# A second buffer for the second pair of weight sums (R) of gate and up

## The chip, the cores and the metric

The kernel runs on one core of one Trainium2 chip. The metric is the device time of one execution in microseconds. A core has engines that work side by side, each through its own instructions in order: TensorE (PE, with its weight loads PEld), VectorE (DVE), ScalarE (ACT), GpSimd (POOL), and SyncE (SP), which here only issues DMAs. They wait for each other through semaphores.

## The reference

One layer of a decoder: a mixer (a state space branch beside a gated delta rule branch), and then a dense SwiGLU block. The change touches only the two first products of that block, gate and up:

```
x = x + rms_norm(mix, norm_mix_post)
f = rms_norm(x, norm_ffn_pre)
f = (silu(f @ w_ffn_gate) * (f @ w_ffn_up)) @ w_ffn_down
x = x + rms_norm(f, norm_ffn_post)
```

There are 2048 prompt tokens and 32 sample tokens, 1024 features, and 2816 hidden columns. The 16 meta tokens run through the mixer only.

## The kernel before

The program is written with tiles and pools. A pool gives each tag a number of buffers; a tile that finds no free buffer waits until the last reader of the oldest one is done. A scheduler then sets the order of the instructions on each engine from the order of the program, the readiness that it computes, and the buffers that are free. So the number of buffers changes not only waits but also the order in which an engine does its work; engines never leave that order on the chip.

**Stages.** Phase one (projections, state space, delta rule) takes the first half of the span. `merge` and `way_out` follow, where the last token tiles are normed, turned to features and written to `f_d`. Then `gate_up` reads `f_d` and writes the hidden rows to `h_d`, and `down` multiplies these by `w_ffn_down`.

**Numbers in two parts.** Each factor of a product is held as a rounded part (`hi`, made by ACT in `fp32r`) and a remainder (`lo`, made by DVE or POOL as the difference). `mm3` (L155) therefore issues three matmuls for one: L158, L159, L160.

**gate_up.** Gate and up are computed by Strassen's scheme in Winograd's form: seven products of half blocks in place of eight. The activations come in three pairs of column blocks of width 348, 348 and 344 (`PAIRS`), the weights in 11 blocks of 256 hidden columns; 33 steps in all. A step of `gate_up_step` does 14 products, seven for gate (i = 0) and seven for up (i = 1), each of 4 x 3 matmuls: 168 matmuls. In the order of the program, with PSUM sums Y, X and Z for each i:

1. Y0 with a11, X0 with a12, Y1 with a11, X1 with a12 (products 1 to 4)
2. Y0 and Y1 with s2 added (5, 6), Z0 with s1 (7), Y0 with s3 added (8), Z1 with s1 (9), Y1 with s3 added (10)
3. Y0 with a22 added (11), Z0 with s4 added (12), Y1 with a22 added (13), Z1 with s4 added (14)

Between the products `snap` (L1537, tile `sn`, ACT) copies a sum out of PSUM before more is added to it; `plus` (L1541, tile `su`, DVE) adds such a copy to another sum; `gated` makes silu with a tanh on ACT (L1546, tile `th`) and a product on DVE (L1547); and `hm` is the hidden row, finished by POOL (L1565, L1579, L1592) or DVE (L1585) and stored by SP (L1550).

**a_parts** prepares the weights of the next step, spread through the present one by `fac()`. For gate and for up it loads the raw block `araw` (1 MB, L1483, two buffers, one each), and makes from it

- a11 and a12: rounded by ACT (L1476, tile `ah`), remainder by DVE (L1477, tile `al`)
- `early(i)`: four sums of 128 x 512 on DVE, S in two halves (L1489, L1490) and R in two halves (L1491, L1492), then s2 and s1 from S (rounded by ACT, remainder by DVE)
- `late(i)`: s3 and s4 from R, and a22 from the raw block (rounded by ACT, remainder by POOL)

The program calls early(0), early(1), late(0), late(1). S and R are tiles of the pool `gs` (L1733), which has one buffer for each tag. R of up can then be written only when `late(0)` has read R of gate, and R of gate for the next step only when `late(1)` has read R of up. The parts s3, s4 and a22 of one i have one buffer as well, so `late(i)` of the next step begins when PE has used the parts of the present one.

Of the kernel before, what the change touches and what calls it, by code (L numbers as in the profile page):

```python
# [7 lines left out]
F32 = mybir.dt.float32  # L8
# [7 lines left out]
P = 128  # L16
# [34 lines left out]
def ap_of(t, off, dims):  # L51
    return bass.AP(tensor=t.tensor, offset=t.offset + off, ap=[list(d) for d in dims])
# [19 lines left out]
class Trunk:  # L72
# [730 lines left out]
    def gdn_special(self):  # L803
# [10 lines left out]
        qn = self.q_norm(sq, SPC)  # L814
        R = slice(32, SPC)

# [19 lines left out]
        for h in range(H):  # L836
            nc.tensor.matmul(pt[R, h], ks[:, h, 1], self.ident, start=True, stop=True)
            nc.tensor.matmul(po[R, h], ks[:, h, 0], self.ident, start=True, stop=True)
        r = self.g2("r")[:SPC]
        v.tensor_copy(r, vc)  # L840
        o = self.g2("o")
        for h in range(H):
            v.scalar_tensor_tensor(r[R, h], pt[R, h], self.c1[R, 0, h:h + 1], vc[R, h], op0=OP.mult, op1=OP.add)
        v.tensor_tensor(o[R], po[R], self.egc[R, 0, :, None].to_broadcast([32, H, P]), op=OP.mult)
        pv = self.gp.tile([P, H, P], F32, tag="gp", name="pv")[:SPC]
# [9 lines left out]
        for h in range(H):  # L855
            nc.tensor.matmul(po[:SPC, h], qk[:, h], vt[:, h], start=True, stop=True)
        v.tensor_add(o[R], o[R], po[R])

# [608 lines left out]
    def a_parts(self, s, out):  # L1467

        nc, v, gp = self.nc, self.nc.vector, self.nc.gpsimd
        flat = lambda t: t.rearrange("p a k m -> p (a k) m")  # L1470
        def parts(i, names, x, eng):
            n = len(names)
            pool = {"a11": self.ae, "s2": self.am[i]}.get(names[0], self.ar)
            hi = pool.tile([P, n, 4, P], F32R, tag=f"{names[0]}{i}h", bufs=1, name="ah")
            lo = pool.tile([P, n, 4, P], F32R, tag=f"{names[0]}{i}l", bufs=1, name="al")
            nc.scalar.activation(flat(hi), x, AF.Copy)  # L1476
            eng.tensor_sub(flat(lo), x, flat(hi).bitcast(F32))  # L1477
            for j, nm in enumerate(names):
                out[i][nm] = hi[:, j], lo[:, j]
        raws, sums = [], [None] * 2  # L1480
        for i, w in enumerate((self.w_fg, self.w_fu)):
            raw = self.gr.tile([P, 8, 256], F32, tag="raw", name="araw")
            nc.sync.dma_start(raw, ap_of(w, 256 * s, [[FF, P], [P * FF, 8], [1, 256]]))  # L1483
            raws.append(raw)
        def early(i):
            a, c = raws[i][:, :, 0:P], raws[i][:, :, P:256]
            S = self.gs.tile([P, 2, 4, P], F32, tag="S", name="S")
            R = self.gs.tile([P, 2, 4, P], F32, tag="R", name="R")
            v.tensor_add(S[:, 1], c[:, 0:4], c[:, 4:8])  # L1489
            v.tensor_sub(S[:, 0], S[:, 1], a[:, 0:4])  # L1490
            v.tensor_sub(R[:, 0], a[:, 0:4], c[:, 0:4])  # L1491
            v.tensor_sub(R[:, 1], a[:, 4:8], S[:, 0])  # L1492
            parts(i, ("s2", "s1"), flat(S), v)
            sums[i] = flat(R)
        def late(i):
            parts(i, ("s3", "s4"), sums[i], gp)
            parts(i, ("a22",), raws[i][:, 4:8, P:256], gp)
        for i in range(2):
            parts(i, ("a11", "a12"), raws[i][:, :, 0:P], v)
            yield  # L1500
        for f in (early, late):
            for i in range(2):
                f(i)
                yield
# [452 lines left out]
```

## Time and profile before

| what | value |
|---|---|
| time, median of 3 runs | 3268.27 us (3264.24 to 3269.39) |
| the profiled execution | 3277.85 us, its span 3275.8 us |
| mean granted TensorE clock | 0.972 |
| gate and up, first to last matmul into `psf` | 1819.8 to 2750.8 us |
| in it: matmuls L158, L159, L160 | 1848 each |
| R's sums L1491, L1492 | 62 each, 128 x 512 |

The profile has one execution. Its page lists busy times by engine, and groups of instructions by line with the idle time of the engine ahead of them and what ended that. Views of the trace give the waits (who waited for whom, total, times, longest), the timeline (start, duration, engine, line, operation, tiles, and in brackets the idle time before it and its releaser) and windows (busy time of each engine in a stretch, with the granted clock and the DMA share). In names, `psf<-xh,ah` reads output from inputs; numbers of buffers are left out, so gate's and up's tiles have one name. Matmuls overlap: one takes some 0.32 us from begin to end, and the next begins after half of that. A releaser is the event that came last by the profile.

### The profile page before, as it was taken

The page shows a single profiled execution, that of the slowest core. Times are in us where ns is not written, and L with a number is a line of the kernel's source. Part 1 is how long each engine was busy: PE and PEld are TensorE (multiplying, and loading weights), DVE is VectorE, ACT ScalarE, POOL GpSimd, SP SyncE. Part 2 cuts the span into 40 slices and gives each one's busy share as a digit, 9 for nine tenths or more (in the row PEclk, how much of TensorE's full clock was granted, in tenths as well). Part 3 has the DMA queues.
Part 4 walks back from the last instruction along what each step waited for, and adds up shares of the span by engine and source line. Part 5 has one row for each costly group of instructions (what it writes and reads, how often), then busy time and mean ns, then how long its engine had stood idle before and what let it go on. Part 6 is the DMA issues. An engine that isn't in the chain of part 4 may idle for free. (4 is left out here: it accounts for less than half of the span.)

```text
span 3275.8 us, 47596 instructions
## 1 busy us (share of the span) xinstructions
PE 3108.8 (95%) x17461; PEld 2729.7 (83%) x17461; DVE 2028.0 (62%) x4674; ACT 1116.7 (34%) x1952; POOL 908.7 (28%) x907
## 2 busy tenths in 40 slices
PE   7998999999989999999999799999999999999998
PEld 6887787877777888888777699999999998888886
DVE  6888854557788645644455766676676664236235
ACT  4643222433333224211243444344444443213211
POOL 1134431112332211201211344434434443212110
PEclk8998998999999999999999899999999999999999
DMA  4335556545556645544555433333332334326223
GB/s 119 120 105 161 145 147 169 121 104 139 158 173 182 168 114 143 165 137 127 181 180 172 149 104 104 104 118 99 100 97 89 102 103 139 125 82 162 78 64 69
DMA packets 460553, 419.30 MB, mean 128 GB/s; under 512 B 112330, under 2 KB 384906, under 8 KB 460320
## 3 DMA queue, kind: packets, MB, share of 16 engines
q1 hardware_dynamic: 450048, 382.18, 40.0%
q0 software_dynamic: 10272, 34.09, 3.8%
q8 instruction: 137, 2.24, 0.3%
q14 instruction: 96, 0.79, 0.1%
HBM read 288.27 MB, written 127.65 MB: 127 GB/s over the span
## 5 line engine op out<-in xcount | busy, mean ns | idle before, releaser
L158 PE MATMUL psf<-xh,ah 128*128 128x348 f32 (+1 forms) x1848 | 598.3, 324 | 27.0 <-ACT sn L1537 20.1
L160 PE MATMUL psf<-xh,al 128*128 128x348 f32 (+1 forms) x1848 | 594.3, 322 | 1.5 <-POOL al L1477 1.5
L159 PE MATMUL psf<-xl,ah 128*128 128x348 f32 (+1 forms) x1848 | 592.9, 321 | 0.0
L145 POOL TENSOR_TENSOR wu<-wr,wu 128x512 fp32r<-128x512 f32 x136 | 218.2, 1607 | 667.5 <-ACT wu L143 618.0
L158 PEld LDWEIGHTS psf<-xh,ah 128*128 128x128 f32 x1848 | 348.4, 189 | 36.5 <-ACT sn L1537 28.7
L160 PEld LDWEIGHTS psf<-xh,al 128*128 128x128 f32 x1848 | 347.9, 188 | 1.8 <-POOL al L1477 1.7
L159 PEld LDWEIGHTS psf<-xl,ah 128*128 128x128 f32 x1848 | 347.9, 188 | 0.0
L158 PE MATMUL psg<-pgh,wu 128*128 128x512 f32 (+2 forms) x800 | 299.6, 374 | 1.2 <-ACT gt L1218 1.2
L1642 PE MATMUL psr<-wu,hh 128*128 128x512 f32 (+2 forms) x748 | 292.4, 391 | 3.7 <-POOL wu L145 3.7
L1641 PE MATMUL psr<-wu,hh 128*128 128x512 f32 (+2 forms) x748 | 290.8, 390 | 2.3 <-ACT wu L143 2.3
L160 PE MATMUL psg<-pgh,wu 128*128 128x512 f32 (+2 forms) x800 | 288.7, 361 | 4.0 <-DVE wu L146 4.0
L159 PE MATMUL psg<-pgl,wu 128*128 128x512 f32 (+2 forms) x800 | 288.0, 360 | 0.0
L1644 PE MATMUL psr<-wu,hl 128*128 128x512 f32 x704 | 274.7, 391 | 0.0
L146 DVE TENSOR_TENSOR wu<-wr,wu 128x512 fp32r<-128x512 f32 x136 | 121.8, 897 | 137.6 <-ACT wu L143 137.2
L143 ACT ACTIVATE wu<-wr 128x1024 fp32r<-128x1024 f32 x136 | 142.6, 1054 | 140.3 <-DMA wr<-w_ffn_down 58.6
L158 PE MATMUL psq<-pgh,wu 128*128 128x512 f32 (+2 forms) x480 | 184.5, 384 | 3.7 <-ACT gt L1218 3.1
L158 PEld LDWEIGHTS psg<-pgh,wu 128*128 128x128 f32 x800 | 154.8, 194 | 29.4 <-issue 9.4
L160 PEld LDWEIGHTS psg<-pgh,wu 128*128 128x128 f32 x800 | 154.8, 194 | 27.0 <-DVE wu L146 4.2
L159 PE MATMUL psq<-pgl,wu 128*128 128x512 f32 (+2 forms) x480 | 175.3, 365 | 0.0
L160 PE MATMUL psq<-pgh,wu 128*128 128x512 f32 (+2 forms) x480 | 174.7, 364 | 0.0
L1477 POOL TENSOR_TENSOR al<-R,ah 128x1024 fp32r<-128x1024 f32 x62 | 162.0, 2613 | 38.5 <-ACT ah L1476 38.5
L159 PEld LDWEIGHTS psg<-pgl,wu 128*128 128x128 f32 x800 | 154.8, 193 | 18.8 <-issue 0.2
(495 smaller groups left out, 6721.1 us busy)
## 6 DMA issues: line engine op xcount, KB each, us to landing
wr<-w_in SPq DMA_DIRECT2D x72, 512.0 KB
araw<-w_ffn_gate SPq DMA_DIRECT2D x31, 1024.0 KB
araw<-w_ffn_up SPq DMA_DIRECT2D x31, 1024.0 KB
wr<-w_ffn_down SPq DMA_DIRECT2D x44, 512.0 KB
zg_d<-gt SPq DMA_DIRECT2D x80, 256.0 KB
h_d<-hm SPq DMA_DIRECT2D x44, 348.0 KB
qkv_d<-cy SPq DMA_DIRECT2D x48, 256.0 KB
hr<-h_d SPq DMA_DIRECT2D x16, 768.0 KB
```

Source lines behind the costliest of these rows:

```text
L143: nc.scalar.activation(hi[:, :n], raw[:, :n], AF.Copy)
L145: nc.gpsimd.tensor_sub(lo[:, :c], raw[:, :c], hi[:, :c].bitcast(F32))
L146: nc.vector.tensor_sub(lo[:, c:n], raw[:, c:n], hi[:, c:n].bitcast(F32))
L158: t.matmul(ps, wh, xh, start=first, stop=False, **kw)
L159: t.matmul(ps, wh, xl, start=False, stop=False, **kw)
L160: t.matmul(ps, wl, xh, start=False, stop=last, **kw)
L1477: eng.tensor_sub(flat(lo), x, flat(hi).bitcast(F32))
L1641: nc.tensor.matmul(ps, hi[:, k, cl], wh[:, cs], start=k == 0, stop=False)
L1642: nc.tensor.matmul(ps, hi[:, k, cl], wl[:, cs], start=False, stop=both and k == n - 1)
L1644: nc.tensor.matmul(ps, lo[:, k, c - c0:c - c0 + r], wh[:, cs], start=False, stop=k == n - 1)
```

## The change

R gets two buffers in place of one. Sums, roundings, products and transfers stay the same in kind, number and size.

```diff
         def early(i):
             a, c = raws[i][:, :, 0:P], raws[i][:, :, P:256]
             S = self.gs.tile([P, 2, 4, P], F32, tag="S", name="S")
-            R = self.gs.tile([P, 2, 4, P], F32, tag="R", name="R")
+            R = self.gs.tile([P, 2, 4, P], F32, tag="R", bufs=2, name="R")
             v.tensor_add(S[:, 1], c[:, 0:4], c[:, 4:8])
             v.tensor_sub(S[:, 0], S[:, 1], a[:, 0:4])
             v.tensor_sub(R[:, 0], a[:, 0:4], c[:, 0:4])
             v.tensor_sub(R[:, 1], a[:, 4:8], S[:, 0])
```

The pool `gs` grows by 4 KB in each partition. The scheduler's order changes at three places.

**DVE, from the end of one step into the next**, in the steady part of the stage. `th_19313` belongs to the end of the step; `araw_19128` is up's raw block and R_19267 up's R for the step that begins; `araw_19392` and `araw_19394` are gate's and up's raw blocks for the step after it, R_19496 and R_19533 their R; `su_19432` adds X0 of the step that begins. Before:

```order
L1547 SCALAR_TENSOR_TENSOR th_19313<-th_19313,su_19311 128x348
L1491 TENSOR_TENSOR R_19267<-araw_19128 128x512
L1492 TENSOR_TENSOR R_19267<-araw_19128,S_19266 128x512
L1585 TENSOR_TENSOR hm_19097<-th_19296,psf_19134 128x348
L1541 TENSOR_TENSOR su_19350<-psf_19239,sn_19200 128x348
L1489 TENSOR_TENSOR S_19495<-araw_19392 128x512
L1490 TENSOR_TENSOR S_19495<-S_19495,araw_19392 128x512
L1491 TENSOR_TENSOR R_19496<-araw_19392 128x512
L1492 TENSOR_TENSOR R_19496<-araw_19392,S_19495 128x512
L1541 TENSOR_TENSOR su_19432<-psf_19379,sn_19377 128x348
L1477 TENSOR_TENSOR al_19397<-araw_19392,ah_19396 128x1024
L1547 SCALAR_TENSOR_TENSOR th_19434<-th_19434,su_19432 128x348
```

The same place with the change:

```order
L1547 SCALAR_TENSOR_TENSOR th_19313<-th_19313,su_19311 128x348
L1585 TENSOR_TENSOR hm_19097<-th_19296,psf_19134 128x348
L1541 TENSOR_TENSOR su_19350<-psf_19239,sn_19200 128x348
L1489 TENSOR_TENSOR S_19495<-araw_19392 128x512
L1491 TENSOR_TENSOR R_19496<-araw_19392 128x512
L1490 TENSOR_TENSOR S_19495<-S_19495,araw_19392 128x512
L1492 TENSOR_TENSOR R_19496<-araw_19392,S_19495 128x512
L1541 TENSOR_TENSOR su_19432<-psf_19379,sn_19377 128x348
L1491 TENSOR_TENSOR R_19533<-araw_19394 128x512
L1477 TENSOR_TENSOR al_19397<-araw_19392,ah_19396 128x1024
L1547 SCALAR_TENSOR_TENSOR th_19434<-th_19434,su_19432 128x348
```

Up's R (R_19267) has left this place; it was done earlier in the step. Where, the next one (R_19533) shows: its first half comes right behind the `su` of X0, and its second half follows in the middle of the step, behind up's S and ahead of the remainder of up's S.

**SP, the loads and stores of one step.** `araw_19392` is gate's raw block, `araw_19394` up's; `hm_19097` is the hidden row that DVE ends (L1585), `hm_19096` the one that POOL ends (L1592). Before:

```order
L1483 DMA araw_19392<-w_ffn_gate 128x8x256
L1483 DMA araw_19394<-w_ffn_up 128x8x256
L1550 DMA h_d_70<-hm_19097 128x696
L1550 DMA h_d_70<-hm_19096 128x696
L1483 DMA araw_19658<-w_ffn_gate 128x8x256
```

With the change:

```order
L1483 DMA araw_19392<-w_ffn_gate 128x8x256
L1550 DMA h_d_70<-hm_19097 128x696
L1483 DMA araw_19394<-w_ffn_up 128x8x256
L1550 DMA h_d_70<-hm_19096 128x696
L1483 DMA araw_19658<-w_ffn_gate 128x8x256
```

Up's load stands behind the first store and ahead of the second one.

**ACT, at the start of the stage**, where the last token tiles of `way_out` (`sq`, and `fo` from the transposes `pst`) run beside the first step of `gate_up`; the first `ah<-S` here is gate's. Before:

```order
L1440 ACTIVATE xh<-t_17704 128x1392
L1476 ACTIVATE ah<-S 128x1024
L274 ACTIVATE fo<-pst,smalls 128x128 x4
L1440 ACTIVATE xh<-fr 128x1392 x3
L1537 ACTIVATE sn<-psf 128x348 x3
L1440 ACTIVATE xh<-t_17704 128x1392
L1546 ACTIVATE th<-su 128x348
L1393 ACTIVATE sq,wss<-xr 128x1024
L274 ACTIVATE fo<-pst,smalls 128x128 x8
L1476 ACTIVATE ah<-S 128x1024
L1476 ACTIVATE ah<-R 128x1024
```

With the change:

```order
L1440 ACTIVATE xh<-t_17704 128x1392
L1440 ACTIVATE xh<-fr 128x1392
L274 ACTIVATE fo<-pst,smalls 128x128 x4
L1440 ACTIVATE xh<-fr 128x1392 x2
L1537 ACTIVATE sn<-psf 128x348 x2
L1393 ACTIVATE sq,wss<-xr 128x1024
L1440 ACTIVATE xh<-t_17704 128x1392
L1546 ACTIVATE th<-su 128x348
L274 ACTIVATE fo<-pst,smalls 128x128 x8
L1476 ACTIVATE ah<-S 128x1024
L1476 ACTIVATE ah<-R 128x1024
```

Gate's first S is now rounded behind the last `fo` instead of ahead of the first ones; on DVE the first S and R of gate and up have moved behind the norm of the last token tile (L1410), and on PE the two products that use gate's S there (Y0 with s2, Z0 with s1) behind that tile's eight transposes. On the other engines and in all steps after the second the order of PE, ACT and POOL is the same in both kernels.

## The prediction

> **What bounds the kernel now.** I read the page from the top: span, busy times, then the costliest groups.
>
> ```profile
> span 3275.8 us, 47596 instructions
> PE 3108.8 (95%) x17461; PEld 2729.7 (83%) x17461; DVE 2028.0 (62%) x4674; ACT 1116.7 (34%) x1952; POOL 908.7 (28%) x907
> L158 PE MATMUL psf<-xh,ah 128*128 128x348 f32 (+1 forms) x1848 | 598.3, 324 | 27.0 <-ACT sn L1537 20.1
> ```
>
> The kernel is bound by TensorE (PE), and nothing here adds or removes a matmul. All that the change can win is time in which PE stands still in the gate and up stage; the third row says that there is some, 27.0 us ahead of the first matmul of a triple, 20.1 of it ended by the snapshot `sn`. How full is PE otherwise? The windows view of a stretch of the stage, and of one of the down stage behind it (columns: PE, PEld, DVE, ACT, POOL busy, clock, DMA):
>
> ```profile
> 2200.00:2300.00 100.00, 97.79 (x608) 96.68 (x607) 68.13 (x83) 40.96 (x64) 46.04 (x26) 1.00 0.36 113
> 2860.00:2960.00 100.00, 100.00 (x443) 82.81 (x442) 39.72 (x51) 20.96 (x21) 19.38 (x11) 1.00 0.32 99
> ```
>
> PE is idle 2.2% in gate and up, at full clock; and the down stage shows that a PE busy for all of 100 us keeps its clock at 1.00, so filling the gaps need not cost clock. Who makes the gaps? The view of waits of that stage, total, times, longest:
>
> ```profile
> PE psf L158 <- ACT sn L1537: 20.1, 31, 1.6
> ACT th L1546 <- DVE su L1541: 168.5, 68, 5.3
> DVE R L1491 <- POOL al L1477: 66.6, 29, 2.3
> ```
>
> 31 waits, about one for each of the stage's 33 steps. Read upward they look like a chain, but totals don't prove one; the timeline of one step does (start, duration, engine, line, idle before it):
>
> ```profile
> 2088.20 0.38 SPq L1483 DMA_DIRECT2D araw<-w_ffn_gate  x1
> 2089.22 2.40 POOL L1477 TENSOR_TENSOR al<-R,ah 128x1024 fp32r<-128x1024 f32 x1 [1.04 <-ACT ah L1476]
> 2089.50 2.49 DVE L1547 SCALAR_TENSOR_TENSOR th<-th,su 128x348 f32<-128x348 f32 x1 [0.85 <-ACT th L1546]
> 2091.92 1.78 DVE L1491 TENSOR_TENSOR R<-araw 128x512 f32<-128x512 f32 x1
> 2093.62 0.68 DVE L1492 TENSOR_TENSOR R<-araw,S 128x512 f32<-128x512 f32 x1
> 2094.36 0.38 SPq L1483 DMA_DIRECT2D araw<-w_ffn_up  x1
> 2094.65 0.51 DVE L1541 TENSOR_TENSOR su<-psf,sn 128x348 f32<-128x348 f32 x1
> 2095.08 0.68 DVE L1489 TENSOR_TENSOR S<-araw 128x512 f32<-128x512 f32 x1
> 2095.23 1.32 POOL L1592 TENSOR_TENSOR hm<-th,su 128x348 f32<-128x348 f32 x1 [2.10 <-DVE su L1541]
> 2096.51 2.86 POOL L1477 TENSOR_TENSOR al<-R,ah 128x1024 fp32r<-128x1024 f32 x1
> 2099.41 0.69 DVE L1491 TENSOR_TENSOR R<-araw 128x512 f32<-128x512 f32 x1 [2.30 <-POOL al L1477]
> 2100.01 0.68 DVE L1492 TENSOR_TENSOR R<-araw,S 128x512 f32<-128x512 f32 x1
> 2100.62 0.51 DVE L1541 TENSOR_TENSOR su<-psf,sn 128x348 f32<-128x348 f32 x1
> 2101.16 0.49 ACT L1546 ACTIVATE th<-su 128x348 f32<-128x348 f32 x1 [4.40 <-DVE su L1541]
> 2101.19 0.32 PE L160 MATMUL psf<-xh,al 128*128 128x348 f32 x1
> 2101.56 0.44 ACT L1537 ACTIVATE sn<-psf 128x348 f32<-128x348 f32 x1
> 2101.90 1.05 ACT L1476 ACTIVATE ah<-araw 128x1024 fp32r<-128x1024 f32 x1
> 2102.06 0.43 PE L158 MATMUL psf<-xh,ah 128*128 128x348 f32 x1 [0.56 <-ACT sn L1537]
> 2102.32 0.32 PE L159 MATMUL psf<-xl,ah 128*128 128x348 f32 x1
> 2113.80 0.32 PE L159 MATMUL psf<-xl,ah 128*128 128x348 f32 x1
> 2129.67 0.43 PE L158 MATMUL psf<-xh,ah 128*128 128x348 f32 x1 [0.54 <-ACT sn L1537]
> ```
>
> From below: PE at 2102.06 adds the sixth product into up's sum, which `sn` must first have copied. ACT could have copied it long before, but stood 4.40 us in front of `th`, whose input `su` is late; `su` is late because DVE, which works in order, waited 2.30 us in front of gate's R. That R waited for the one buffer, which up's R of the step before held until POOL had read it (2096.51 + 2.86). And that read is late because up's R was written only at 2091.92, behind POOL's reading of gate's R. So the one buffer makes gate and up take turns, and a turn is too long for the step by a little.
>
> **The price of the wait.** Between matmuls lie (2113.80 - 2102.32)/72 = 0.1594 us, so a step of 168 should take 26.79 us. It takes 2129.67 - 2102.06 = 27.61: 0.82 us lost, 0.71 as the gap itself (2101.19 to 2102.06, less one beat) and 0.1 as the slow restart (2102.06 to 2102.32). In the third pair of columns (width 344):
>
> ```profile
> 2680.07 0.42 PE L158 MATMUL psf<-xh,ah 128*128 128x344 f32 x1 [0.72 <-ACT sn L1537]
> 2680.33 0.32 PE L159 MATMUL psf<-xl,ah 128*128 128x344 f32 x1
> 2691.63 0.32 PE L159 MATMUL psf<-xl,ah 128*128 128x344 f32 x1
> 2707.46 0.42 PE L158 MATMUL psf<-xh,ah 128*128 128x344 f32 x1 [0.72 <-ACT sn L1537]
> ```
>
> a beat is 11.30/72 = 0.157, a step should be 26.37 and is 27.39: 1.02 lost. Of the 31 waits 22 lie in the first two pairs and 9 in the third: 22 x 0.82 + 9 x 1.02 = **27.2 us**, all that can be won in the steady steps. The least that the same rows allow, the bare idle time, is 20.1.
>
> **The change part by part.** No instruction is added or taken away; 31 x 4 sums, roundings and remainders are done as before. Three things move.
>
> *R no longer takes turns.* By the order, DVE now does after up's last product `hm`, `su`, then S, R, S, R of gate (four sums), then `su` of gate, then the first sum of up's R. When does `su` begin, and when must it? Its followers take 0.54 (to `th`), 0.40 (to `sn`) and 0.50 (to PE) by the rows above, 1.44 in all. PE would be ready at 2101.19 + 0.16 = 2101.35, so `su` must begin by 2099.91; now it is 2100.62, 0.71 too late, which is the gap. Up's R (1.70 + 0.60) has left the place ahead of `hm`, so DVE is ready for S at about 2092.8. S needs gate's load, issued at 2088.20. What a load takes is seen where one is waited for:
>
> ```profile
> 1853.34 0.37 SPq L1483 DMA_DIRECT2D araw<-w_ffn_gate  x1
> 1858.92 0.71 DVE L1489 TENSOR_TENSOR S<-araw 128x512 f32<-128x512 f32 x1 [1.03 <-DMA araw<-w_ffn_gate]
> ```
>
> 5.6 us, so S begins at 2093.8. Four sums at 0.60 each (2099.41 to 2100.01) give `su` at 2096.2. A sum beside a busy POOL takes up to 1.70 (2091.92 to 2093.62); four such give 2100.6, no better than now. I take a value between: POOL has two instructions there, the end of `hm` (0.7 at most after 2093.8) and up's remainder (2.40 at 2089.22), and each can hold up one sum, not four: 2093.8 + 2.4 + 3.1 = 2099.3 at the latest, 0.6 us before the limit, 3.7 at the earliest. So the gap closes in every such step, and what is late next has more room: ACT's `sn` is then bound by its own product.
>
> The row of 2089.50 shows this hold-up: `th` took 2.49 us and ended 0.37 after POOL's read of gate's R (2089.22 + 2.40); the sums at 2099.41 and 2100.01, with POOL idle, took 0.69 and 0.68. [...]
>
> *Up's first sum and its load.* That sum now stands ahead of gate's a11 remainder, `th` and up's `su` on DVE and waits for up's load. On SP that load is now queued behind the store of the first `hm`, not ahead of both stores:
>
> ```profile
> araw<-w_ffn_up SPq DMA_DIRECT2D x31, 1024.0 KB
> h_d<-hm SPq DMA_DIRECT2D x44, 348.0 KB
> ```
>
> The store waits for `hm`, which comes 2.3 us earlier since up's R left the place ahead of it; so I let the load go out no later than today's 2094.36, beside a store of 348 KB. At 5.6 x 1372/1024 = 7.5 us (an estimate by bytes) it lands by 2101.9. DVE may stand there up to 5 us; behind it wait only POOL's `hm` and remainders for the next step, and DVE is busy 68 of 100 us. What PE could notice is ACT's rounding of up's a11 (2101.90), since the snapshot of gate's sum stands behind it. It is due before the eighth product, at 2101.35 + 2 x 1.91 = 2105.2; less 1.05, 0.44 and 0.50 the load may land at 2103.2. Cost: nothing, with 1.3 us to spare.
>
> *The start of the stage.* The allocator's larger pool moves the first S and R behind the last token tile's norm, as the order of ACT shows, and two products with them. Here the trace has
>
> ```profile
> 1848.63 0.66 PE L158 MATMUL psf<-xh,ah 128*128 128x348 f32 x1 [6.48 <-ACT ah L1476]
> 1859.14 0.43 PE L160 MATMUL psf<-xh,al 128*128 128x348 f32 x1 [1.45 <-POOL al L1477]
> ```
>
> PE waits here until 1848.63 anyway. Doing two products (2 x 1.91 us) only after that would lose 3.8 us. Against this DVE reaches the end of that norm with some 4.8 us less work ahead of it (six sums of 0.6 and a remainder of 1.2 leave their place), and the wait of 1.45 for R's turn goes. I take 0, between a loss of 4 and a gain of 6.
>
> **Sum.** 3277.85 (the profiled execution: its span of 3275.8 and 2 us around it) - 27 = 3251. That execution lies 9.6 us above the median of the runs, so for the median 3268.27 - 27 = **3241 us**. With 20.1 to 27.2 for the steps and -4 to +6 for the start its own range is 3235 to 3252.
>
> **Rivals.** *POOL's hold-up eats it* (chance 0.12): if more than two of the four sums are held up, `su` begins between 2099.9 and 2100.6 and a part of the gap stays; half of it gives 3268 - 13.6 = 3255. For it: R took 1.78 and `th` 2.49 in the rows above. Against it: POOL has only two instructions in that stretch.
>
> *Another wait takes its place* (0.07): PE's gap is closed by another cause of the same length, or the two snapshots at the changes of pairs stay and the start loses 4 and more: 3262 to 3274, no change. Against it: the group's 27.0 us of L158 are 20.1 for `sn` and 6.48 in the start; there is 0.4 left for anything else.
>
> *Up's load comes too late* (0.05), and the kernel is slower: the load, now behind a store, lands after 2103.2; then ACT's rounding holds the snapshot and PE waits at the eighth product. At 2104.1 the loss equals the 0.82 of today; at 2105.0 it is 31 x 1.8 = 56 us, less the 27: 3268 + 29 = 3297. For it: the order on SP. Against it: the load would need 10.6 us from today's issue, and 5.6 was seen.
>
> That the change does nothing is excluded, as DVE's order is another one.
>
> **Chances and range.** Forecast 0.76, part 0.12, no change 0.07, slower 0.05. The forecast's 3235 to 3252 with the partial case to 3257 holds about 0.8. Faster by over 0.2% (6.5 us, about what a measurement of this kernel can tell from no change): 0.88; within: 0.07; slower: 0.05.
>
> **What will show it.** Right: the row "PE psf L158 <- ACT sn" falls from 31 waits to a few, "DVE R L1491 <- POOL al" from 66.6 us to near nothing, a step of the second pair takes 26.8 us, and windows of the stage show PE above 99%. R L1491 may wait for "DMA araw<-w_ffn_up" instead, at no cost. Wrong: a period that stays at 27.6; a new releaser ahead of L158, L159 or L160; a first wait in the stage that ends later than 1848.63 by more than 4 us; or a clock under 1.00 once PE has no gaps.

## The result, and the profile after

| | before | changed |
|---|---|---|
| median, us | 3266.26 (3263.95 to 3269.39, 4 runs) | 3239.36 (3235.94 to 3243.47, 4 runs) |
| profiled execution, its span | 3277.85, 3275.8 | 3235.94, 3233.8 |
| first to last matmul into `psf` | 930.98 | 904.28 |
| the same, first two steps | 78.14 | 77.84 |

The ratio is 0.9907 (95% interval 0.9891 to 0.9924): faster by 26.9 us at the medians. The two spans differ by more, 42 us, but 15 of these lie ahead of the stage: the first matmul into `psf` starts at 1804.81 in place of 1819.79, in a part of the program where the order is the same, so that is the run and not the change (in the traces of the thirteen kernels of the table below that matmul starts between 1803.99 and 1819.79 us, with one buffer or two). Therefore the stage itself, first to last matmul into `psf`, from start to start, is what I compare below; steps are read by taking every 168th matmul of it. From the page of the changed kernel, and its windows view of the stretch that the prediction quotes:

```profile
span 3233.8 us, 47558 instructions
PE 3087.9 (95%) x17461; PEld 2720.1 (84%) x17461; DVE 2049.3 (63%) x4674; ACT 1126.3 (35%) x1952; POOL 895.9 (28%) x907
L158 PE MATMUL psf<-xh,ah 128*128 128x348 f32 (+1 forms) x1848 | 595.3, 322 | 8.2 <-ACT ah L1476 5.1
2200.00:2300.00 100.00, 100.00 (x629) 100.00 (x628) 72.36 (x85) 44.13 (x66) 45.43 (x27) 1.00 0.37 114
```

PE now does 629 matmuls in 100 us in place of 608, at full clock; the 27.0 us of idle time ahead of L158 have become 8.2, all in the first step. The waits of the stage:

```profile
PE psf L158 <- ACT sn L1537: 1.1, 1, 1.1
ACT th L1546 <- DVE su L1541: 119.6, 66, 4.8
DVE S L1489 <- DMA araw<-w_ffn_gate: 25.7, 29, 2.6
DVE R L1491 <- DMA araw<-w_ffn_up: 6.6, 13, 1.4
```

PE's 31 waits for the snapshot are one, and R's wait for POOL (66.6 us) is gone from the list. `th` still waits 119.6 us for `su`, which now costs nothing. One step, from the timeline (it starts at 2231.14, the sixth product at 2240.72):

```profile
2227.59 0.37 SPq L1483 DMA_DIRECT2D araw<-w_ffn_gate  x1
2230.96 1.57 POOL L1477 TENSOR_TENSOR al<-araw,ah 128x512 fp32r<-128x512 f32 x1
2231.83 0.33 SPq L1550 DMA_DIRECT2D h_d<-hm  x1
2232.50 0.93 POOL L1592 TENSOR_TENSOR hm<-th,su 128x348 f32<-128x348 f32 x1
2232.56 0.37 SPq L1483 DMA_DIRECT2D araw<-w_ffn_up  x1
2233.06 0.91 DVE L1489 TENSOR_TENSOR S<-araw 128x512 f32<-128x512 f32 x1 [0.83 <-DMA araw<-w_ffn_gate]
2233.39 2.85 POOL L1477 TENSOR_TENSOR al<-R,ah 128x1024 fp32r<-128x1024 f32 x1
2233.89 2.89 DVE L1491 TENSOR_TENSOR R<-araw 128x512 f32<-128x512 f32 x1
2236.71 0.68 DVE L1490 TENSOR_TENSOR S<-S,araw 128x512 f32<-128x512 f32 x1
2237.43 0.69 DVE L1492 TENSOR_TENSOR R<-araw,S 128x512 f32<-128x512 f32 x1
2238.04 0.51 DVE L1541 TENSOR_TENSOR su<-psf,sn 128x348 f32<-128x348 f32 x1
2238.58 0.50 ACT L1546 ACTIVATE th<-su 128x348 f32<-128x348 f32 x1 [2.46 <-DVE su L1541]
2238.83 0.69 DVE L1491 TENSOR_TENSOR R<-araw 128x512 f32<-128x512 f32 x1 [0.28 <-DMA araw<-w_ffn_up]
2238.98 0.44 ACT L1537 ACTIVATE sn<-psf 128x348 f32<-128x348 f32 x1
2240.72 0.32 PE L158 MATMUL psf<-xh,ah 128*128 128x348 f32 x1
```

Gate's R no longer waits for POOL before it starts. It takes 2.89 us instead, and ends half a microsecond behind POOL's instruction that began before it; the other three sums take 0.68 to 0.91. Even so `su` starts 6.90 us into the step, where it started 8.85 us into it before. The snapshot ends at 2239.42; PE needs it 1.24 us later (2240.72, less the 0.06 from the end of a snapshot to the matmul).

Every step of the first two pairs from the second on now takes 26.81 us, every step of the third 26.41. Before, an ordinary step of the first two pairs took 27.6 (27.9 in a few), one of the third 27.39; the second step and the last one of a pair took longer (29.4 and 28.5), and the one behind a change of pairs already ran at 26.81 or 26.41.

### The profile page after: what moved, and what is told of

Read it like the earlier page. It is cut to its first block, busy times and chain, and to the rows that moved or that the text cites. A ratio compares the mean times of both kernels' runs of the same rounds, so it can differ in the third digit from the quotient of the medians.

```text
span 3233.8 us, 47558 instructions
## 1 busy us (share of the span) xinstructions
PE 3087.9 (95%) x17461; PEld 2720.1 (84%) x17461; DVE 2049.3 (63%) x4674; ACT 1126.3 (35%) x1952; POOL 895.9 (28%) x907
## 4 chain that ended last, share of the span: by engine, by line
PE 61%; issue 14%; DVE 14%; DMA 6%; POOL 3%; ACT 2%; SPq 1%; POOLq 0%; DVEq 0%; ACTq 0%
PE psf L160 9%; PE psf L158 9%; PE psf L159 9%; PE psg L158 2%; PE psr L1642 2%; PE psr L1644 2%; PE psg L160 2%; PE psr L1641 2%; PE psg L159 2%; DVE cy L386 2%; DMA wr<-w_ffn_down 1%; PE psq L158 1%; PE psq L160 1%; PE psq L159 1%; DVE bt L625 1%
## 5 line engine op out<-in xcount | busy, mean ns | idle before, releaser
L158 PE MATMUL psf<-xh,ah 128*128 128x348 f32 (+1 forms) x1848 | 595.3, 322 | 8.2 <-ACT ah L1476 5.1
L158 PEld LDWEIGHTS psf<-xh,ah 128*128 128x128 f32 x1848 | 348.8, 189 | 9.4 <-ACT ah L1476 5.8
L158 PE MATMUL psg<-pgh,wu 128*128 128x512 f32 (+2 forms) x800 | 301.2, 376 | 1.2 <-ACT gt L1218 1.2
L158 PE MATMUL psq<-pgh,wu 128*128 128x512 f32 (+2 forms) x480 | 183.4, 382 | 4.3 <-ACT gt L1218 3.8
L158 PEld LDWEIGHTS psg<-pgh,wu 128*128 128x128 f32 x800 | 155.8, 195 | 26.6 <-issue 6.1
```

The costliest lines, as they stand in the source:

```text
L158: t.matmul(ps, wh, xh, start=first, stop=False, **kw)
```

## The experiments

All medians and ratios are against runs of the kernel before on the same chip; the stage and the steps are from one trace of each (us). Medians of kernels whose stages agree within 1 us differ by up to 5, as the part ahead of the stage varies from run to run, so the stage is the finer measure.

| kernel | median | ratio, 95% interval | stage | first two steps | a step of pair two / three |
|---|---|---|---|---|---|
| before | 3264.43 to 3268.88 in the four groups | 1 | 930.98 | 78.14 | 27.63 / 27.39 |
| changed | 3239.36 | 0.9907, 0.9891 to 0.9924 | 904.28 | 77.84 | 26.81 / 26.41 |
| s_two | 3264.90 | 0.999, 0.998 to 1.0 | 929.82 | 77.24 | 27.63 / 27.39 |
| pad | 3266.62 | 0.9994, 0.9984 to 1.0004 | 929.44 | 77.12 | 27.63 / 27.39 |
| r_apart | 3242.05 | 0.9917, 0.9902 to 0.9932 | 903.65 | 77.21 | 26.81 / 26.41 |
| sn_first | 3244.72 | 0.9925, 0.991 to 0.9939 | 904.85 | 78.33 | 26.81 / 26.41 |
| dve | 3238.91 | 0.9912, 0.9898 to 0.9925 | 901.53 | 75.09 | 26.81 / 26.41 |
| pool2b | 3382.94 | 1.0349, 1.0321 to 1.0377 | 1046.07 | 84.75 | 30.04 to 32.63 / 31.2 to 32.6 |
| su1 | 3240.20 | 0.9914, 0.99 to 0.9927 | 903.59 | 76.57 | 26.81 / 26.41 |
| su2 | 3241.68 | 0.9915, 0.9901 to 0.9929 | 904.99 | 78.49 | 26.81 / 26.41 |
| sd2 | 3250.18 | 0.9952, 0.9932 to 0.9972 | 913.56 | 79.43 | 27.12 / 26.41 |
| pool2 | 3271.70 | 1.0015, 1.0002 to 1.0028 | 936.38 | 78.48 | 27.82 / 27.57 |
| load | 3246.83 | 0.9926, 0.9913 to 0.994 | 907.02 | 76.95 | 26.81 / 26.41 to 27.58 |

### Is it R's buffer? (s_two, pad, r_apart)

**s_two**, the second buffer for S:

```diff
-            S = self.gs.tile([P, 2, 4, P], F32, tag="S", name="S")
+            S = self.gs.tile([P, 2, 4, P], F32, tag="S", bufs=2, name="S")
             R = self.gs.tile([P, 2, 4, P], F32, tag="R", name="R")
```

> S gets the second buffer in place of R. Theory: R still takes turns, R L1491 still waits for POOL some 60 us in all and PE for the snapshot in about 31 steps of 27.6 us; with the start as in the padded kernel 3268, ratio 1.0005. Rival (any looser buffer of the sums, or the other order that it brings, closes the gap): near 3239, ratio 0.992.

Its waits:

```profile
DVE R L1491 <- POOL al L1477: 69.3, 30, 2.7
PE psf L158 <- ACT sn L1537: 20.4, 31, 2.2
```

As the theory had it: the wait for POOL and the 31 waits of PE stay. A second buffer for S is worth nothing here.

**pad**, one buffer, and an unused tile of R's size in the pool:

```diff
-            R = self.gs.tile([P, 2, 4, P], F32, tag="R", name="R")
+            R = self.gs.tile([P, 2, 4, P], F32, tag="R", name="R"); self.gs.tile([P, 2, 4, P], F32, tag="pad", name="pad")
```

> R has one buffer, and the pool gs gets an unused tile of the size of R, so the start of the stage is ordered as with the change, and the steady steps as before. Theory: the wait of R for POOL and PE's gap of 0.82 us stay in every step, the first step takes some 51 us: 2.3 us over the kernel before, near 3268.5, ratio 1.0007. Rival (the place in memory or the start makes the gain): near 3239, ratio 0.992.

The steady steps stay at 27.63 and 27.39, so a larger pool without a second R makes no gain in them. The other half of the expectation failed: the first two steps take 77.12 us, 1.0 less than before and not 2.3 more.

**r_apart**, a buffer each for gate and up, and the start ordered as before:

```diff
-            R = self.gs.tile([P, 2, 4, P], F32, tag="R", name="R")
+            R = (self.gs, self.ar)[i].tile([P, 2, 4, P], F32, tag="R", bufs=1, name="R")
```

> Gate's R stays in the pool gs, up's R gets the one buffer of its own in the pool ar; the first S and R keep their place at the start of the stage as before the change. Theory (the steady gain is the end of R's turns, and the changed start costs what its first step shows, 51.03 against 48.70 us): every step after the first takes 26.8 or 26.4 us as with the change, the first one 48.7, so 2.3 us under the changed kernel, near 3237 us, ratio to the kernel before 0.991. Rival A (the first step's 2.3 us come from elsewhere): 3239.5 as the changed kernel. Rival B (the gain needs the two buffers that rotate between gate and up): steps of 27.6 and 3266.

The steady gain is whole, so two buffers that rotate aren't needed; what counts is that gate and up no longer share one. But the 2.3 us are not to be had: the stage is 0.6 shorter than in the changed kernel. I had read the start from its first step alone. The rows of the first matmuls of steps one to three, before:

```profile
1819.79 0.40 PE L158 MATMUL psf<-xh,ah 128*128 128x348 f32 x1
1868.48 0.32 PE L158 MATMUL psf<-xh,ah 128*128 128x348 f32 x1
1897.92 0.32 PE L158 MATMUL psf<-xh,ah 128*128 128x348 f32 x1
```

That is 48.7 and 29.4 us. The changed kernel has 51.0 and 26.8: what its first step loses, its second gives back.

### Is it the chain that the prediction drew? (sn_first, pool2b, dve)

**sn_first** cuts the last link: one buffer, R waits as before, but the snapshot stands ahead of the late tanh.

```diff
-        def plus(ps, t):
+        def plus(ps, t, u=None):
...
-            v.tensor_add(o, ps, t)
+            u is None or v.tensor_copy(o[:, 0:1], u[:, 0:1]); v.tensor_add(o, ps, t)
...
-        t = gated(plus(X[0], s1[0]))
+        t = gated(plus(X[0], s1[0], s1[1]))
```

> R has one buffer. The first snapshot of up is put ahead of the tanh of X0 on ACT, by one more DVE instruction, a copy of one column of that snapshot into the tile of X0's sum before the sum is made; what the copy writes is overwritten. Theory (PE's gap is ACT's queue: the snapshot has its input but stands behind a late tanh): R still waits for POOL about 60 us, su begins even later (10.2 us into the step against 8.9), yet PE has no gap at the sixth product, steps of 26.8 and 26.4 us, 27 us won, near 3239, ratio 0.992; the next thing due on ACT, the snapshot of gate's sum for the eighth product, has some 0.6 us to spare. Rival (R's turns hold PE by the parts s3, s4, or by whatever else follows from R): no gain, 3266; or the eighth product waits in place of the sixth: between 3239 and 3266.

Its waits, and rows of a step that starts at 2210.05 from its timeline:

```profile
DVE R L1491 <- POOL al L1477: 70.3, 30, 3.5
PE psf L158 <- ACT sn L1537: 1.3, 1, 1.3
```

```profile
2216.05 0.46 ACT L1537 ACTIVATE sn<-psf 128x348 f32<-128x348 f32 x1 [1.00 <-PE psf L160]
2217.69 0.69 DVE L1491 TENSOR_TENSOR R<-araw 128x512 f32<-128x512 f32 x1 [2.30 <-POOL al L1477]
2220.22 0.52 DVE L1541 TENSOR_TENSOR su<-psf,sn 128x348 f32<-128x348 f32 x1
2220.78 0.49 ACT L1546 ACTIVATE th<-su 128x348 f32<-128x348 f32 x1 [4.27 <-DVE su L1541]
```

This is the plainest of the runs. R waits for POOL as long as ever, `su` starts 10.17 us into the step, 1.3 later than in the kernel before, and PE has no gap, since the snapshot is taken 3.1 us ahead of its need. R's turn never held PE itself. It made DVE late, that made a tanh late, and PE waited because its snapshot stood behind that tanh in ACT's queue.

**pool2b** makes the turn longer: the kernel before, POOL's remainder from up's R made twice.

```diff
-            eng.tensor_sub(flat(lo), x, flat(hi).bitcast(F32))
+            for _ in range(2 if (i, names[0]) == (1, "s3") else 1): eng.tensor_sub(flat(lo), x, flat(hi).bitcast(F32))
```

> The kernel before (one buffer), with the same doubled POOL instruction. Theory (the turns of the one buffer set the step: R of gate waits until POOL has read up's R): each turn gets 2.4 to 2.9 us longer, and so does PE's gap in each of 31 steps, steps of 30.0 to 30.5 us in pair two: 74 to 90 us over the kernel before, near 3348. Rival (the turn has slack elsewhere that takes it up): under 30 us more.

```profile
DVE R L1491 <- POOL al L1477: 137.8, 30, 4.8
PE psf L158 <- ACT sn L1537: 87.6, 29, 3.4
```

R's wait grew from 2.30 to 4.6 us (137.8 / 30), and from matmul start to matmul start PE's gap from 0.87 to 3.28, by 2.41 us, the length of one POOL instruction (2.40 at 2089.22 in the prediction's rows). A step that has only this takes 27.63 + 2.41 = 30.04, inside the 30.0 to 30.5 expected. But most steps are 1.3 or 2.6 us longer, and the kernel lost 118 us, more than the 74 to 90 expected. That is the granted clock of PE (0.72 in a stretch about one such gap), which the last section shows.

**dve** makes the turn shorter: one buffer, the remainders from R on DVE.

```diff
-            parts(i, ("s3", "s4"), sums[i], gp)
+            parts(i, ("s3", "s4"), sums[i], v)
```

> R has one buffer. The remainder of the parts s3 and s4 (al from R) is made on DVE in place of POOL, 62 instructions of some 1.24 us there instead of 2.4 to 2.9 on POOL: each turn of R gets shorter by 1.2 to 1.6 us, and has no other engine between but ACT. Theory (a turn is too long by 0.71 us only): R waits for nothing that costs, su begins near 6 us into the step against 8.9 before, no PE gap, 27 to 29 us won, near 3238, ratio 0.991. Rival (DVE is what makes su late, by its load): 2.4 us more work in each step keep or widen the gap, 3266 or more.

Steps of 26.81 and 26.41, as expected, without a second buffer; `su` starts 6.39 us into the step (5.8 in pair three), and R's wait has left the list of waits. Its page:

```profile
PE 3088.1 (95%) x17461; PEld 2721.1 (84%) x17461; DVE 2038.2 (63%) x4736; ACT 1125.1 (35%) x1952; POOL 754.6 (23%) x845
```

DVE has 62 instructions more, 94.9 us of work (1.226 each by the median, 1.53 by the mean), yet is busy only 10 us longer than before (2028.0). The gate product `th` from `su`, which took up to 2.50 us beside POOL's read of R, now takes 0.52 at most, 59 us less in all, and the second half of S takes 20 us less; R's two halves together are as dear as before. So this run takes away a hold-up as well as a part of the turn, and by itself it doesn't tell the two apart; R's wait of 2.30 us, now gone, is nearly all of the 2.46 by which `su` comes earlier.

### How much room is there? (su1, su2, sd2, pool2)

**su1** and **su2** make the sum `su` of X0 two and three times, with n of 2 and 3:

```diff
-        def plus(ps, t):
+        def plus(ps, t, n=1):
...
-            v.tensor_add(o, ps, t)
+            for _ in range(n): v.tensor_add(o, ps, t)
...
-        t = gated(plus(X[0], s1[0]))
+        t = gated(plus(X[0], s1[0], 2))
```

> The changed kernel, with the sum su of X0 made twice (the same values into the same tile), one after the other: the tanh behind it comes 0.53 us later in each step. In the changed kernel the snapshot for the sixth product ends 1.24 us earlier than PE needs it in pairs one and two, 1.05 to 1.11 in pair three (0.68 in one step). Theory: 0.53 is inside that room, so no PE gap and no change against the changed kernel: 3239, within 2 us. Rival (the room is used up, since the hold-up of R eats most of it in a part of the steps): some ms of the steps get a gap of up to 0.5, 3240 to 3255.

> The changed kernel, with the sum su of X0 made three times; on DVE the remainder of gate's a11 (1.24 us) now stands ahead of the last of them, so the tanh comes 2.3 us later in each step. Theory: 2.3 is 1.06 over the room in 20 steps and 1.2 over it in 9, and each gap has a slow restart of 0.1: 20 x 1.16 + 9 x 1.3 = 35 us lost against the changed kernel, 3274, so slower than the kernel before; PE L158 waits for the snapshot L1537 again. Rival (the sixth product has more room than I read, or the wait moves the whole step and DVE with it): 3239 to 3250.

su1 came out as expected: 0.55 of the room is used and 0.69 left in a step of pair two, and only the steps at the two changes of pairs grow, by 0.3 and 0.2. su2 did not. Its timeline, in a step that starts near 2231:

```profile
2236.96 0.46 ACT L1537 ACTIVATE sn<-psf 128x348 f32<-128x348 f32 x1 [1.02 <-PE psf L160]
2239.97 0.51 DVE L1541 TENSOR_TENSOR su<-psf,sn 128x348 f32<-128x348 f32 x1
2240.52 0.50 ACT L1546 ACTIVATE th<-su 128x348 f32<-128x348 f32 x1 [3.10 <-DVE su L1541]
```

The tanh is 2.1 us later, near the 2.3 reckoned, but the scheduler, which reckons with the longer chain too, has put the snapshot ahead of it. This run is sn_first over again and says nothing of the room. So a longer chain in the program need not show up as a longer wait. Why the scheduler left the snapshot behind the late tanh in the kernel before (perhaps because it doesn't reckon with DVE standing still for POOL) no run shows.

**sd2** therefore adds DVE work that leaves ACT's order alone:

```diff
-            v.tensor_sub(S[:, 0], S[:, 1], a[:, 0:4])
+            for _ in range(3 if i == 0 else 1): v.tensor_sub(S[:, 0], S[:, 1], a[:, 0:4])
```

> The changed kernel, with gate's S L1490 made three times (the same values), ahead of su on DVE; the order of tanh and snapshot on ACT stays as in the changed kernel. Theory: su begins 2 x 0.69 = 1.38 us later, 0.14 more than the room of 1.24 in 20 steps and 0.3 more than that of 1.05 to 1.11 in 9: steps of 26.95 to 27.05 and 26.7 to 26.8, 5 to 9 us over the changed kernel, near 3246. Rival (the room is larger than read, or the scheduler's other order gives it back): steps of 26.81 and 26.41, no change.

Two sums cost 1.45 us. In the first two pairs `su` starts at 8.34 us and the steps take 27.12, a little over the 26.95 to 27.05 expected, so the gap is back: 0.2 us idle and 0.1 of slow restart, where 1.45 - 1.24 = 0.21 was to be seen. The limit is where it was read. In the third pair the order differs (the second half of R stands behind `su` there), which I hadn't looked for: `su` starts at 7.7, and the gap is not there.

**pool2** is the changed kernel with pool2b's edit.

> The changed kernel, with the remainder of up's s3 and s4 (al from R) made twice on POOL, the same values, one after the other; the order on PE, DVE, ACT and SP stays the same. In the changed kernel one of DVE's sums (R L1491) is held up by this POOL instruction until it ends. Theory (each POOL instruction is paid once by DVE, and the changed kernel has 1.24 us of room in pairs one and two and 1.05 to 1.11 in pair three): the second one holds up one more sum, su begins 2.4 to 3.0 us later, PE's gap at the sixth product comes back with 1.2 to 1.8 us: 20 steps by 1.27 to 1.87 and 9 by 1.4 to 2.0, so 38 to 55 us over the changed kernel, 3277 to 3294, slower than the kernel before, although R has two buffers. Rival (the long sum is chance or a fixed cost of R's first half, and POOL's work costs DVE only a share of its time): no gap or one of under 0.5, 3239 to 3252.

A step that starts at 2229.55:

```profile
2231.75 5.66 POOL L1477 TENSOR_TENSOR al<-R,ah 128x1024 fp32r<-128x1024 f32 x2
2232.26 2.90 DVE L1491 TENSOR_TENSOR R<-araw 128x512 f32<-128x512 f32 x1
2235.08 2.88 DVE L1490 TENSOR_TENSOR S<-S,araw 128x512 f32<-128x512 f32 x1
2237.99 0.69 DVE L1492 TENSOR_TENSOR R<-araw,S 128x512 f32<-128x512 f32 x1
2238.60 0.51 DVE L1541 TENSOR_TENSOR su<-psf,sn 128x348 f32<-128x348 f32 x1
```

Two POOL instructions, two dear sums, 2.90 and 2.88 us in place of 0.69: one for each. `su` is 2.15 us later (9.05), which is 0.91 past the room; the steps grow by 1.01 and 1.16, and with both buffers in place the kernel is a little slower than before (1.0015, 1.0002 to 1.0028). The loss of 32 us is a little under the 38 to 55 expected, because the expectation took POOL's 2.4 to 3.0 us as the delay; a held-up sum takes 2.88 in place of 0.69, which is 2.2. Even so it is the rival of the prediction that came nearest: one more POOL instruction of that size in this place takes all of the gain.

### Up's load (load)

```diff
-            nc.sync.dma_start(raw, ap_of(w, 256 * s, [[FF, P], [P * FF, 8], [1, 256]]))
+            nc.sync.dma_start(raw, ap_of(w, 256 * s, [[FF, P], [P * FF, 8], [1, 256]])); i and nc.sync.dma_start(raw, ap_of(w, 256 * s, [[FF, P], [P * FF, 8], [1, 256]]))
```

> The changed kernel, with up's raw block loaded twice, the second time behind the first and with the same values, so that it lands some 6 us later, 13 to 14 us into the step; ACT's order then has the snapshot of gate's sum ahead of the rounding of up's a11. Theory (up's load has room, since what needs it is due in the next step): DVE waits longer at up's first R, PE has no gap, 3239 within 3 us. Rival (the load is close to the path): PE waits at the sixth to tenth product, or for ah from up's a11 at the start of the next step, 1 us or more in each of 31 steps: 3270 or more.

```profile
DVE R L1491 <- DMA araw<-w_ffn_up: 107.7, 27, 6.6
DVE S L1489 <- DMA araw<-w_ffn_gate: 64.0, 29, 4.5
PE psf L158 <- ACT sn L1537: 3.8, 5, 2.0
```

DVE's wait for the load grew from 6.6 to 107.7 us, ACT's to 100, and most steps stay at 26.81 or 26.41. Five of the third pair take 0.2 to 1.2 more, and the stage is 2.7 longer than in the changed kernel. The way is not the one that the rival named: where PE's gap is longest (0.92 us idle, up to 2652.28), gate's load goes out 0.43 us ahead of the step in place of 3.46, gate's S waits 4.53 us for it, and `su` starts 9.10 us into the step, past its limit. Why gate's load goes out so late is not shown. The median is 7.5 higher, more than the 3 that I allowed; the intervals of the two ratios overlap, and how much of the rest is the load stays open. The rival's 1 us in each of 31 steps is out.

## Why the prediction was right, point by point

- **PE's gaps are what can be won, 27.2 us.** Right: 26.7 in the stage, 26.9 at the medians. The count of 22 and 9 waits was right, but three of the 22 are not the steady wait that was priced: by PE's gaps 28 lie in ordinary steps (19 and 9), the others in the second step and at the two changes of pairs. Their gaps went too, so the sum held. From the third step on the first two pairs gained 17.6 (0.93 each, with the changes of pairs) and the third 8.7 (0.97 each). The beat was right as well: 26.79 and 26.37 worked out, 26.81 and 26.41 measured.
- **The chain from R over `su` and `th` to `sn`.** Right, and shown link by link: pool2b moves its first link and PE's gap follows by the same 2.41 us; dve shortens the turn (and frees DVE of a hold-up) and the gap is gone; sn_first cuts only the last link, and the gap is gone while R still waits.
- **When `su` begins.** 7.5 us into the step at the latest and 3.1 us earlier at best, said the prediction (2099.3 and 2096.2 in a step that starts at 2091.77); it was 6.90. The worst case had two POOL instructions paid in full. The long one was, 2.2 us over a plain sum; the end of POOL's `hm` cost 0.2. The limit, 8.14 us by the prediction's rows, was 8.14 (6.90 + 1.24), and sd2 found the gap just beyond it. In pair three the room was 1.05.
- **POOL's hold-up, once for each instruction.** That each of POOL's two instructions holds up one sum, not four, was the author's estimate, with one row behind it (2089.50: `th` took 2.49 us and ended 0.37 after POOL's instruction). The traces show it: in the changed kernel each of the 28 ordinary steps has one sum of 2.88 to 2.90 us beside POOL's 2.85 to 2.87, ended 0.55 after it, and the step of pool2 above has two (2.90 and 2.88 us).
- **Up's load.** Right in what it costs, nothing. It is issued 1.42 us into the step, earlier than the 2.6 of the kernel before, 0.03 after POOL's remainder of a22 ended (2230.96 + 1.57); the store ahead of it had gone out 0.7 earlier and held nothing. Before, it went out 0.06 after up's R, a reader of the same block, ended (2093.62 + 0.68): with R done earlier the load is free to go earlier, which the prediction didn't see. It lands 6.3 us after its issue, where 7.5 was reckoned.
- **The start of the stage.** Taken as 0 between -4 and +6; the first two steps gained 0.3, a loss of 2.3 in the first and a gain of 2.6 in the second. The terms behind the 0 were not measured apart, and two kernels with two buffers (su1, su2) differ by 1.9 us there, so that it came out near 0 is in part luck.
- **The rivals.** "POOL's hold-up eats it" fell by 1.24 us in a step of the first two pairs and 1.05 in one of the third, and pool2 shows that it would have decided. "Another wait" and "up's load too late" did not come about. Clock: 1.00 in all windows from 1900 to 2700 us, as said; in the first step it was lower at times (0.86 in the window from 1800 to 1850 us; last section).

No version tried beats the changed kernel by more than can be measured. The stages of dve and r_apart are 2.8 and 0.6 us shorter, all of it in the first two steps; with PE at 100% in the others there is nothing left here but the start.

## What to carry to other kernels

A buffer is worth what the wait at the end of its chain costs, and the chain may pass through queues that have nothing to do with it: follow it to the engine that sets the time, then ask which link is cheapest to cut. Here four different cuts (a second buffer, a buffer apart, a shorter turn, one instruction put ahead of another) each took 26 to 29 us from the stage. And ask how much room the change leaves: 1.24 us were enough for all of the gain, and in pool2 one more POOL instruction beside DVE, with `su` 2.15 us later, used them up, and the gain with them.

## What the runs showed of the hardware

In pool2b PE's gap of 3.28 us (2.96 of bare idle time; 3.43 and 3.11 in pair three) was followed in 26 of 29 cases by some nine or more matmuls at about half the rate. Two stretches about such a gap, by the windows view, and the first matmuls after the first one:

```profile
2277.00:2283.20 6.20, 3.24 (x12) 3.02 (x11) 4.85 (x7) 2.14 (x4) 2.34 (x2) 0.72 0.04 13
2308.00:2314.40 6.40, 3.44 (x22) 3.16 (x21) 4.85 (x7) 2.60 (x5) 2.57 (x2) 1.00 0.08 30
```

```profile
2280.18 0.66 PE L158 MATMUL psf<-xh,ah 128*128 128x348 f32 x1 [2.96 <-ACT sn L1537]
2280.64 0.49 PE L159 MATMUL psf<-xl,ah 128*128 128x348 f32 x1
2280.93 0.49 PE L160 MATMUL psf<-xh,al 128*128 128x348 f32 x1
```

The granted clock is 0.72 in the first and 1.00 in the second, after gaps of the same length (2.96 us idle); in the first, matmuls follow each other by 0.29 us in place of 0.16. From the third step on pool2b has 316 matmuls with such a distance to the next (0.24 to 0.40 us), the kernel before 30: 286 x 0.13 = 37 us. From there on it is 108 us longer than the kernel before, and 28 gaps that grew by 2.41 make 67 of it; by this estimate the clock accounts for nearly all of the other 41. The changed kernel shows it too, near the end of its first step, right behind a wait of PE of 2.02 us (up to 1851.51):

```profile
1852.06:1855.47 3.41, 3.41 (x14) 3.41 (x13) 2.93 (x6) 1.60 (x4) 0.93 (x1) 0.50 0.81 257
```

Outside pool2b's 29 gaps, PE stood idle nine times for 1.96 to 2.84 us at full clock in the stages of the thirteen kernels; eight of these were followed by a clock of 0.50 and one (2.01 us, in su1) was not. None of the 141 idle times of 0.4 to 1.72 us was. So in this stage a wait of some 2 us or more mostly cost more than its length, and one of up to 1.7 us didn't.
